# Order of high and low products within a quarter of a column tile, in a decoder layer on one Trainium2 core

## The chip, the cores and the metric

One core of a Trainium2 chip runs the whole kernel. TensorE multiplies, ScalarE (ACT) and VectorE (DVE) work element by element, GpSimd (POOL) takes a few element-wise steps and some DMAs, and SyncE (SP) issues most DMAs. The metric is the device time of one execution in microseconds (us); smaller is better.

## The reference, cut to what matters

One decoder layer on 256 tokens of 2048 numbers. A combined input projection gives latent queries, a shared key/value latent, gates, indexer queries and keys and the input of a recurrence; branch A is sparse attention with 16 heads, branch B a gated linear recurrence; both are projected, gated, added, projected once more, added to the input and normalised.

```python
proj = jnp.einsum('btd,dc->btc', x, w_in[l])
(q_lat, c_kv, attn_gate, q_idx, k_idx, w_idx,
 x_rnn, rnn_gate, g_a, g_b) = jnp.split(proj, SPLIT_POINTS, axis=-1)
...
attn = _sparse_attention(q_lat, c_kv, q_idx, k_idx, w_idx, rel_bias, w_uv[l])
branch_a = jnp.einsum('btc,cd->btd', attn * jax.nn.silu(attn_gate), w_branch_a[l])
h = _rglru(x_rnn, conv_w[l], conv_b[l], w_gate_a[l], b_gate_a[l], w_gate_x[l], b_gate_x[l], lru_lambda[l])
branch_b = jnp.einsum('btc,cd->btd', h * jax.nn.silu(rnn_gate), w_branch_b[l])
merged = jax.nn.sigmoid(g_a) * branch_a + jax.nn.sigmoid(g_b) * branch_b
sub = jnp.einsum('btd,de->bte', merged, w_out[l])
x = _layernorm(ALPHA * x + sub, ln_g[l], ln_b[l])
```

## The kernel before, in words

All numbers are float32. For the products each operand is written as a sum of a high and a low part of 12 significant bits each (`hi_of`, line 84, on ScalarE; `lo_of`, line 87, on VectorE). A product then is high x high + high x low + low x high. The activations of all 256 tokens stand as [high 256 | low 256], 512 columns, for each of the 16 slices k of the 2048 inputs: `xs[:, k, :]`, or `us[k]` for the two branch projections.

The large weights come as *column tiles*: 2048 rows (16 slices k of 128) by 128 columns. There are 148 of them, in the order of `col_jobs` (line 51): 4 of indexer queries (qi), 16 attention gates (ag), 32 queries (q), 16 + 16 of gate and projection of branch A (ga, ba), 16 recurrence inputs (xr), gates and recurrence gates (gb, rg), 16 of the projection of branch B (bb). A column tile arrives in two halves of 8 slices (`load_to`, line 148, DMAs of 512 KB on SP's queue); each half is split into hi and lo (`split_to`, line 161), with five buffers for each part.

The loop over column tiles (line 720) goes through four *quarters* of four slices each. For a slice, `mm3` (line 183) issues two products into one accumulator of 512 columns (`ps_...`, one of four banks): the weights' high part (stationary) times all 512 columns, and the weights' low part times the left 256 columns only. So the right half collects high x low, the left half high x high + low x high.

```python
        if last:
            nc.tensor.matmul(ps[:, :T], lo, rhs[:, :T], start=first, stop=False)
            nc.tensor.matmul(ps, hi, rhs, start=False, stop=True)
        else:
            nc.tensor.matmul(ps, hi, rhs, start=first, stop=False)
            nc.tensor.matmul(ps[:, :T], lo, rhs[:, :T], start=False, stop=False)
```

Behind each quarter stands `tick(t)` (line 112): it emits one more step of whatever other work is due, an agenda written by hand: the evacuation of finished tiles (`evac`, line 261: ScalarE copies the right half, VectorE adds the left), the indexer (products pss), attention heads (products psl, transposes pspT, products pspv), the heads' values (psv), the recurrence's gates (psg). Their TensorE products come between two quarters. Behind a first or third quarter the next half is split and a further half is loaded. The order on each engine is the order in which the program issues.

Ahead of the column tiles stands phase A (keys, latent, first indexer queries), which also uses `mm3` (line 257). Behind them stands the output projection (`products`, line 771): into pso and the first psz it issues 512-column products only, into the last psz 256-column ones only. Then come residual and norm.

Of the kernel before, what the change touches and what calls it, by code (L numbers as in the profile page):

```python
# [16 lines left out]
DRAM = bass.MemoryType.DRAM  # L17

P = 128
T = 256  # L20
DM = 2048
KT = DM // P
# [6 lines left out]
EPS = 1e-5  # L29
# [19 lines left out]


def col_jobs():
    """The column tiles in the order in which the tensor engine takes them."""
    jobs = [("qi", i) for i in range(4, 8)]
    jobs += [("ag", i) for i in range(16)]
    jobs += [("q", i) for i in range(2 * NH)]
    jobs += [("ga", i) for i in range(16)] + [("ba", i) for i in range(16)]
    jobs += [("xr", i) for i in range(16)]
    jobs += [("gb", i) for i in range(14)] + [("rg", i) for i in range(16)] + [("gb", 14), ("gb", 15)]
    jobs += [("bb", i) for i in range(16)]
    return jobs  # L60
# [3 lines left out]
def layer(ctx, tc, ar, out):  # L64
# [20 lines left out]
        nc.scalar.activation(hi, src, AF.Copy)  # L85

    def lo_of(lo, src, hi):
        """src = hi + lo exactly, each of 12 significant bits."""
        nc.vector.tensor_sub(lo, src, f(hi))  # L89

    def acc_tile(name):
# [11 lines left out]
    def gate_tile(name):  # L103
        return gt.tile([P, T], F32, name=name, tag="gate", bufs=32)

# [1 line left out]
    agenda = {}  # L107

    def spawn(t, gen):
# [7 lines left out]
                continue  # L117
            spawn(t + (wait or 1), gen)

# [1 line left out]
    zero = const.tile([P, P], mybir.dt.bfloat16, name="zero")  # L121
    nc.vector.memset(zero, 0.0)
    one = const.tile([P, 1], F32, name="one")
# [14 lines left out]
    dv = dram.tile([NH, VL], F32, name="dv")  # L138
    dz = dram.tile([P, NH, VL], F32, name="dz")

# [1 line left out]
    halves = [("t", j, s) for j in range(NJ) for s in range(2)]  # L142
    halves += [("o", ec, pc) for ec in range(4) for pc in range(8)]
    NO = 2 * NJ
# [36 lines left out]
            st["split"] += 1  # L181

    def mm3(ps, hi, lo, rhs, first, last):
        """hi x [hi | lo] into all columns of ps, lo x hi into the left ones."""
        if last:
            nc.tensor.matmul(ps[:, :T], lo, rhs[:, :T], start=first, stop=False)
            nc.tensor.matmul(ps, hi, rhs, start=False, stop=True)
        else:
            nc.tensor.matmul(ps, hi, rhs, start=first, stop=False)  # L189
            nc.tensor.matmul(ps[:, :T], lo, rhs[:, :T], start=False, stop=False)  # L190

    def mm6(o, pairs):
        """o (256 columns) = the sum over pairs of (hi, lo) stationary x (hi, lo) moving."""
        n = len(pairs)
        for i, ((sh, sl), (mh, ml)) in enumerate(pairs):
            nc.tensor.matmul(o, sh, mh, start=i == 0, stop=False)
            nc.tensor.matmul(o, sh, ml, start=False, stop=False)
            nc.tensor.matmul(o, sl, mh, start=False, stop=i == n - 1)

# [1 line left out]
    warm = aux_tile("warm")  # L201
    for i in range(32):
        nc.tensor.matmul(warm[:, :P], zero, zero, start=True, stop=True)
# [55 lines left out]
                split_to(k - 11)  # L259

    def evac(ps, name, dst=None):
        """Both halves of a product's accumulator, added."""
        r = tmp_tile(f"r_{name}", "r")
        nc.scalar.activation(r, ps[:, T:], AF.Copy)
        yield
        if dst is None:
            dst = tmp_tile(f"s_{name}", "s")
        nc.vector.tensor_add(dst, ps[:, :T], r)
        return dst

    def rsqrt(ssq, tmp, scale):
        """-2 / sqrt(ssq * scale + EPS): the table's root and a Newton step."""
        v, y, z = tmp
        nc.scalar.activation(z, ssq, AF.Sqrt, scale=scale, bias=eps)
        nc.vector.tensor_scalar(v, ssq, scale, EPS, op0=OP.mult, op1=OP.add)
        yield
        nc.vector.reciprocal(y, z)
        yield
        nc.vector.tensor_mul(z, y, y)
        nc.vector.tensor_mul(z, z, v)  # L280
        nc.vector.scalar_tensor_tensor(v, z, -3.0, y, op0=OP.add, op1=OP.mult)
        return v

    gt = ctx.enter_context(pool("gt"))

    # the keys that the tokens of tile 1 - r can see
    W = (T, P)

# [1 line left out]
    idx_stack = ExitStack()  # L290
    idx = idx_stack.enter_context(pool("idx", side="right"))
    ks = {}
# [48 lines left out]
            lo_of(cT[d][:, T:], ps[:, d, :], cT[d][:, :T])  # L341

    def post_qi(i, ps):
        """Two heads' queries: each has its high part on one half of the partitions and its low
        part on the other, for keys that stand on both."""
        s = yield from evac(ps, f"qi{i}")
        yield
        q = qis[i] = slot(f"qis{i}")
        heads = [(slice(0, DI), slice(DI, P), slice(0, T)), (slice(DI, P), slice(0, DI), slice(T, 2 * T))]
        for own, other, c in heads:  # L350
            hi_of(q[own, c], s[own, :])
        yield
        for own, other, c in heads:
            lo_of(q[other, c], s[own, :], q[own, c])

    def scores(i):
        """Of the first token tile only the first half of the keys is causal: the first two
        quarters of pss hold q x hi and q x lo of those keys."""
        q, k = qis[i], ks[0].rearrange("p (a s) -> p a s", a=2)
        pss = [aux_tile(f"pss{i}_{g}") for g in range(2)]  # L360
        for g in range(2):
            nc.tensor.matmul(pss[g][:, :T], q[:, g * T:g * T + P], k[:, :, :P], start=True, stop=True)
            for e in range(2):
                nc.tensor.matmul(pss[g][:, T:], q[:, g * T + P:(g + 1) * T], k[:, e, :], start=e == 0, stop=e == 1)
        yield
        rl = []
        for g in range(2):
            rl.append(idx.tile([P, 2 * T], F32, name=f"rl{i}_{g}", tag="rl", bufs=4))
            nc.scalar.activation(rl[g][:, P:T], pss[g][:, P:T], AF.Copy)
            nc.scalar.activation(rl[g][:, T:], pss[g][:, T:], AF.Relu)  # L370
        yield
        for g in range(2):
            nc.vector.tensor_add(rl[g][:, :P], pss[g][:, :P], rl[g][:, P:T])
        yield
        for g in range(2):
            nc.gpsimd.tensor_scalar(rl[g][:, :P], rl[g][:, :P], 0.0, None, op0=OP.max)
        for g in range(2):
            yield
            for t in range(2):
                h = 2 * i + g  # L380
                c = slice(0, W[1 - t])
                prev = causal[:, t, c] if h == 0 else score[t][:, c]
                nc.vector.scalar_tensor_tensor(score[t][:, c], rl[g][:, t * T:t * T + W[1 - t]], wi[:, t, h:h + 1],
                                               prev, op0=OP.mult, op1=OP.add)
# [18 lines left out]
            c = slice(0, wide[t])  # L403
            nc.vector.tensor_add(mask[:, 1 - t, c], score2[t][:, c], causal[:, t, c])

# [1 line left out]
    def rel():  # L407
        oh = idx.tile([32, VL], F32, name="oh")
        nc.sync.dma_start(oh, ar["onehot"])
# [19 lines left out]
            nc.gpsimd.tensor_add(b[:, r, :W[r]], b[:, r, :W[r]], mask[:, r, :W[r]])  # L429
        bias[h] = b  # L430

# [1 line left out]
    vs = {}  # L433

    def values(g):
# [18 lines left out]
        lo_of(lo, ps, hi)  # L454
        vs[g] = (hi, lo)

# [1 line left out]
    qs = {}  # L458

    def post_q(i, ps):  # L460
# [72 lines left out]
        yield  # L533
        lo_of(us[h][:, T:], u, us[h][:, :T])

# [1 line left out]
    gates = {}  # L537

    def post_ag(i, ps):
# [34 lines left out]
        yield  # L574
        lo_of(xs[:, d, T:], g, xs[:, d, :T])

# [1 line left out]
    def lru_consts():  # L578
        """c8 = 8 softplus(-lambda), nc8 = -c8; log1p by the series of artanh."""
        lam = params[:, 7, :]  # L580
        t = const.tile([P, 4, 16], F32, name="lru")
        m, e, z, q = (t[:, i, :] for i in range(4))
# [70 lines left out]
        nc.vector.tensor_mul(t[:, T:], t[:, T:], xc)  # L653

    def decay(n):
        """a = exp(-x) in place of r, 1 - a^2 = tanh(x) (1 + a^2), x = 8 r softplus(-lambda)."""
        r, w = ri[n][:, :T], v[:, n, :]
        nc.scalar.activation(w, r, AF.Tanh, scale=c8[:, n:n + 1])
        nc.scalar.activation(r, r, AF.Exp, scale=nc8[:, n:n + 1])
        yield  # L660
        a2 = tmp_tile(f"a2{n}", "u", 2)
        nc.scalar.activation(a2, r, AF.Square)
        yield
        nc.vector.scalar_tensor_tensor(w, a2, 1.0, w, op0=OP.add, op1=OP.mult)
# [28 lines left out]
    posts = {"qi": post_qi, "ag": post_ag, "q": post_q, "ga": post_ga, "ba": post_ba, "xr": post_xr,  # L693
             "rg": post_rg, "gb": post_gb, "bb": post_bb}

# [1 line left out]
    E0, D0, A0, C0, G0 = (4 * at[k, 0] for k in ("ag", "q", "ga", "xr", "gb"))  # L697
    spawn(0, post_a())
    for i in range(4):
# [16 lines left out]
        spawn(G0 + 50 + q, roots(q))  # L716
    FIN = 4 * at["bb", 4]

# [1 line left out]
    for j, (kind, i) in enumerate(jobs):  # L720
        rhs = us if kind in ("ba", "bb") else {k: xs[:, k, :] for k in range(KT)}
        ps = acc_tile(f"ps_{kind}{i}")
        for qt in range(4):
# [20 lines left out]
                for e in range(2):  # L744
                    nc.gpsimd.dma_start(y[e], ar["xres"][e * P:(e + 1) * P, :])
            hi, lo = parts[t // 2]
            for kk in range(4):
                k = qt * 4 + kk
                c = slice((k % 8) * P, (k % 8 + 1) * P)
                mm3(ps, hi[:, c], lo[:, c], rhs[k], k == 0, k == KT - 1)  # L750
            if qt % 2:
                parts.pop(t // 2)
            tick(t)
# [2 lines left out]
                load_to(t // 2 + 9)  # L756
        spawn(4 * j + 4, posts[kind](i, ps))

# [1 line left out]
    st6 = [fin.tile([P, 5, 6], F32, name=f"st{t}") for t in range(2)]  # L760
    mv = [fin.tile([P, 2], F32, name=f"mv{t}") for t in range(2)]
    tmp = [fin.tile([P, 4], F32, name=f"lt{t}") for t in range(2)]

    def piece(n):
        """The rows 2 d and 2 d + 1 (of 128) of w_out's column chunk, as (hi, lo) each."""
        p = parts[n]
        if isinstance(p, list):
            return p
        return [tuple(w[:, i * 512:(i + 1) * 512] for w in p) for i in range(2)]
# [18 lines left out]
            yield  # L788

    def normalise(t, ne):  # L790
        """(y - mean) g' (-2 / std) + b, with g' = -g / 2: most columns on the vector engine,
        the rest between the scalar and the Pool engine."""
        mean = mv[t][:, 0:1]
        nc.vector.bn_aggr(mv[t], st6[t][:, :ne, :])
        cuts = [slice(0, 384), slice(384, 896), slice(896, 1280), slice(1280, 1536)]
# [114 lines left out]
```

## Time and profile before

| | |
|---|---|
| median of 3 runs | 1050.54 us (1047.70 to 1051.33) |
| span of the profiled execution | 1046.6 us |
| its own time | not listed apart from the three runs, which lie 1.1 to 4.7 us above its span |
| TensorE busy | 1029.8 us, 98% of the span, 5944 products |
| TensorE weight loads (PEld) | 901.2 us, beside the products |
| VectorE busy | 709.3 us, 68% |
| ScalarE busy | 571.6 us, 55% |
| GpSimd busy | 87.4 us, 8% |
| DMA | 201.49 MB, mean 193 GB/s |

The span runs from the first instruction to the last. A product's time in the timeline is modelled from its start and overlaps the next product's; the distance from one start to the next is what it occupies TensorE for, and is called its *slot* below. A weight load (LDWEIGHTS, engine PEld) goes beside the product ahead. A row of the summary by stretches gives, for each engine, busy us and in brackets the number of instructions that begin in the stretch.

### The profile page before, as it was taken

To read this page: it belongs to the slowest core of one execution; us is meant where nothing else is said; L and a number is where in the kernel's file an instruction comes from. 1 tells how busy PE (TensorE), PEld (TensorE's weight loads), DVE (VectorE), ACT (ScalarE), POOL (GpSimd) and SP (SyncE) were. 2 spreads that over 40 slices of the span, in tenths; PEclk is the share of its full clock that TensorE was granted. 3 is DMA by queue.
4 is the path that set the end of the run, shared out by engine and by line. 5 is a ranking of instruction groups with operands and counts; after the bars stand their busy time and mean duration, and the time that the engine had idled before them with its cause. 6 is when DMAs were issued, how large, how long until landed. Compare 5 with 4: busy or idle time off the path is not lost.

```text
span 1046.6 us, 16107 instructions
## 1 busy us (share of the span) xinstructions
PE 1029.8 (98%) x5944; PEld 901.2 (86%) x5944; DVE 709.3 (68%) x1246; ACT 571.6 (55%) x989; POOL 87.4 (8%) x121
## 2 busy tenths in 40 slices
PE   8999999999999999999999999999999999999995
PEld 7988888888888888888888888888888888888885
DVE  4667586677677676545555788856577777675666
ACT  5666355555655657544444555578755545554341
POOL 1003211111111100000000000000230020000002
PEclk9999999999999999999999999999999999999998
DMA  8745856755656654656566766555656677656652
GB/s 275 262 145 178 288 180 218 235 174 177 191 170 183 191 163 145 196 182 194 185 184 186 218 188 191 163 174 187 180 186 191 188 266 261 195 186 186 197 162 81
DMA packets 60575, 201.49 MB, mean 193 GB/s; under 512 B 6577, under 2 KB 13617, under 8 KB 59857
## 3 DMA queue, kind: packets, MB, share of 16 engines
q1 hardware_dynamic: 59120, 190.89, 59.2%
q0 software_dynamic: 944, 8.88, 2.3%
q8 instruction: 47, 0.77, 0.3%
q10 hardware_dynamic: 432, 0.70, 0.2%
q14 instruction: 32, 0.25, 0.1%
HBM read 198.31 MB, written 6.32 MB: 196 GB/s over the span
## 4 chain that ended last, share of the span: by engine, by line
PE 92%; DVE 2%; DMA 2%; ACT 2%; issue 1%; POOL 0%; SPq 0%; DVEq 0%; ACTq 0%; POOLq 0%
PE ps_q L189 11%; PE ps_q L190 5%; PE ps_rg L189 5%; PE ps_ba L189 5%; PE ps_bb L189 5%; PE ps_gb L189 5%; PE ps_xr L189 5%; PE ps_ga L189 5%; PE ps_xr L190 3%; PE ps_gb L190 3%; PE ps_bb L190 3%; PE ps_ba L190 3%; PE ps_ga L190 3%; PE ps_rg L190 3%; PE pso L776 2%; PE pso L777 2%
## 5 line engine op out<-in xcount | busy, mean ns | idle before, releaser
L89 DVE TENSOR_TENSOR lo<-raw,hi 128x1024 fp32r<-128x1024 f32 x324 | 401.2, 1239 | 296.7 <-ACT hi L85 296.3
L85 ACT ACTIVATE hi<-raw 128x1024 fp32r<-128x1024 f32 x324 | 340.8, 1053 | 98.1 <-PE pso L778 29.7
L189 PE MATMUL ps_q<-xs,hi 128*128 128x512 f32 x480 | 172.0, 396 | 0.0
L190 PE MATMUL ps_q<-xs,lo 128*128 128x256 f32 x480 | 134.5, 280 | 0.0
L189 PEld LDWEIGHTS ps_q<-xs,hi 128*128 128x128 f32 x480 | 90.1, 188 | 18.0
L190 PEld LDWEIGHTS ps_q<-xs,lo 128*128 128x128 f32 x480 | 90.6, 189 | 1.5
L189 PE MATMUL ps_xr<-xs,hi 128*128 128x512 f32 x240 | 86.0, 398 | 0.0
L189 PE MATMUL ps_ga<-xs,hi 128*128 128x512 f32 x240 | 85.7, 398 | 0.0
L189 PE MATMUL ps_ag<-xs,hi 128*128 128x512 f32 x240 | 85.6, 397 | 0.0
L189 PE MATMUL ps_gb<-xs,hi 128*128 128x512 f32 x240 | 85.6, 398 | 0.0
L189 PE MATMUL ps_ba<-ua,hi 128*128 128x512 f32 x240 | 85.4, 399 | 0.0
L189 PE MATMUL ps_rg<-xs,hi 128*128 128x512 f32 x240 | 85.4, 399 | 0.0
L189 PE MATMUL ps_bb<-ub,hi 128*128 128x512 f32 x240 | 85.4, 399 | 0.0
L190 PE MATMUL ps_ag<-xs,lo 128*128 128x256 f32 x240 | 67.6, 282 | 0.7 <-DVE lo L89 0.6
L190 PE MATMUL ps_xr<-xs,lo 128*128 128x256 f32 x240 | 67.4, 281 | 0.0
L190 PE MATMUL ps_gb<-xs,lo 128*128 128x256 f32 x240 | 67.4, 281 | 0.0
L190 PE MATMUL ps_ba<-ua,lo 128*128 128x256 f32 x240 | 67.4, 281 | 0.0
L190 PE MATMUL ps_rg<-xs,lo 128*128 128x256 f32 x240 | 67.4, 281 | 0.0
L190 PE MATMUL ps_bb<-ub,lo 128*128 128x256 f32 x240 | 67.4, 281 | 0.0
L190 PE MATMUL ps_ga<-xs,lo 128*128 128x256 f32 x240 | 67.3, 281 | 0.0
L189 PEld LDWEIGHTS ps_rg<-xs,hi 128*128 128x128 f32 x240 | 45.1, 188 | 10.4
L189 PEld LDWEIGHTS ps_ba<-ua,hi 128*128 128x128 f32 x240 | 45.1, 188 | 10.4
(306 smaller groups left out, 2091.3 us busy)
## 6 DMA issues: line engine op xcount, KB each, us to landing
raw<-in_wt SPq DMA_DIRECT2D x296, 512.0 KB, 4.1
raw<-in_wo SPq DMA_DIRECT2D x32, 512.0 KB, 4.3
wr<-in_wA SPq DMA_DIRECT2D x15, 424.0 KB, 4.9
dz<-dv POOLq DMA_DIRECT2D x1, 4096.0 KB, 18.8
bias<-dz SPq DMA_DIRECT2D x16, 256.0 KB, 4.4
xr<-in_xT SPq DMA_DIRECT2D x16, 128.0 KB, 4.7
uvr<-in_wuv SPq DMA_DIRECT2D x8, 256.0 KB, 4.1
wgr<-in_wg SPq DMA_DIRECT2D x4, 512.0 KB, 4.8
```

Source lines behind the costliest of these rows:

```text
L85: nc.scalar.activation(hi, src, AF.Copy)
L89: nc.vector.tensor_sub(lo, src, f(hi))
L189: nc.tensor.matmul(ps, hi, rhs, start=first, stop=False)
L190: nc.tensor.matmul(ps[:, :T], lo, rhs[:, :T], start=False, stop=False)
L776: nc.tensor.matmul(o, mh, hi, start=d == 0, stop=False)
L777: nc.tensor.matmul(o, mh, lo, start=False, stop=False)
```

## The change

In the loop over column tiles a new function `mm12` takes the place of the four calls of `mm3`. It issues the same eight products of a quarter, grouped by part: in the first and third quarter of a tile the four high products, then the four low ones; in the second and fourth the four low ones, then the four high ones. The accumulator is opened by the high product of slice 0 and closed by the high product of slice 15, as before. Phase A keeps `mm3`. Besides that only comments and docstrings are gone, so line numbers move by 13 or less.

```diff
+    def mm12(ps, hi, lo, rhs, qt):
+
+
+        def some(w, cols):
+            for k in range(4 * qt, 4 * qt + 4):
+                c = slice((k % 8) * P, (k % 8 + 1) * P)
+                nc.tensor.matmul(ps[:, :cols], w[:, c], rhs[k][:, :cols], start=k == 0 and w is hi,
+                                 stop=k == KT - 1 and w is hi)
+
+        order = [(hi, 2 * T), (lo, T)]
+        for w, cols in order if qt % 2 == 0 else order[::-1]:
+            some(w, cols)
+
...
             hi, lo = parts[t // 2]
-            for kk in range(4):
-                k = qt * 4 + kk
-                c = slice((k % 8) * P, (k % 8 + 1) * P)
-                mm3(ps, hi[:, c], lo[:, c], rhs[k], k == 0, k == KT - 1)
+            mm12(ps, hi, lo, rhs, qt)
             if qt % 2:
                 parts.pop(t // 2)
             tick(t)
```

On TensorE, the first quarter of the first tile of branch A's projection (ba0; ua0 to ua3 are the activations of slices 0 to 3, hi136 and lo136 the two parts of the weight half), in the program before:

```order
L189 MATMUL ps_ba0_5417<-ua0_2518,hi136_5327 128x512
L190 MATMUL ps_ba0_5417<-ua0_2518,lo136_5328 128x256
L189 MATMUL ps_ba0_5417<-ua1_2686,hi136_5327 128x512
L190 MATMUL ps_ba0_5417<-ua1_2686,lo136_5328 128x256
L189 MATMUL ps_ba0_5417<-ua2_2866,hi136_5327 128x512
L190 MATMUL ps_ba0_5417<-ua2_2866,lo136_5328 128x256
L189 MATMUL ps_ba0_5417<-ua3_3026,hi136_5327 128x512
L190 MATMUL ps_ba0_5417<-ua3_3026,lo136_5328 128x256
```

and now:

```order
L198 MATMUL ps_ba0_5417<-ua0_2518,hi136_5327 128x512
L198 MATMUL ps_ba0_5417<-ua1_2686,hi136_5327 128x512
L198 MATMUL ps_ba0_5417<-ua2_2866,hi136_5327 128x512
L198 MATMUL ps_ba0_5417<-ua3_3026,hi136_5327 128x512
L198 MATMUL ps_ba0_5417<-ua0_2518,lo136_5328 128x256
L198 MATMUL ps_ba0_5417<-ua1_2686,lo136_5328 128x256
L198 MATMUL ps_ba0_5417<-ua2_2866,lo136_5328 128x256
L198 MATMUL ps_ba0_5417<-ua3_3026,lo136_5328 128x256
```

The eight products are the same; the low ones have moved behind the four high ones.

The end of that tile and the start of the next (ba1), before:

```order
L189 MATMUL ps_ba0_5417<-ua13_4673,hi137_5352 128x512
L190 MATMUL ps_ba0_5417<-ua13_4673,lo137_5353 128x256
L189 MATMUL ps_ba0_5417<-ua14_4808,hi137_5352 128x512
L190 MATMUL ps_ba0_5417<-ua14_4808,lo137_5353 128x256
L186 MATMUL ps_ba0_5417<-ua15_4930,lo137_5353 128x256
L187 MATMUL ps_ba0_5417<-ua15_4930,hi137_5352 128x512
L189 MATMUL ps_ba1_5468<-ua0_2518,hi138_5378 128x512
L190 MATMUL ps_ba1_5468<-ua0_2518,lo138_5379 128x256
L189 MATMUL ps_ba1_5468<-ua1_2686,hi138_5378 128x512
L190 MATMUL ps_ba1_5468<-ua1_2686,lo138_5379 128x256
```

and now:

```order
L198 MATMUL ps_ba0_5417<-ua12_4519,lo137_5353 128x256
L198 MATMUL ps_ba0_5417<-ua13_4673,lo137_5353 128x256
L198 MATMUL ps_ba0_5417<-ua14_4808,lo137_5353 128x256
L198 MATMUL ps_ba0_5417<-ua15_4930,lo137_5353 128x256
L198 MATMUL ps_ba0_5417<-ua12_4519,hi137_5352 128x512
L198 MATMUL ps_ba0_5417<-ua13_4673,hi137_5352 128x512
L198 MATMUL ps_ba0_5417<-ua14_4808,hi137_5352 128x512
L198 MATMUL ps_ba0_5417<-ua15_4930,hi137_5352 128x512
L198 MATMUL ps_ba1_5468<-ua0_2518,hi138_5378 128x512
L198 MATMUL ps_ba1_5468<-ua1_2686,hi138_5378 128x512
L198 MATMUL ps_ba1_5468<-ua2_2866,hi138_5378 128x512
L198 MATMUL ps_ba1_5468<-ua3_3026,hi138_5378 128x512
```

Before, two products of one size stand together only here; now four low and then eight high ones do.

A whole tile of the recurrence inputs now (equal rows are counted together; xs are the activations of all slices):

```order
L198 MATMUL ps_xr_6327<-xs,hi_6235 128x512 x4
L198 MATMUL ps_xr_6327<-xs,lo_6236 128x256 x8
L198 MATMUL ps_xr_6327<-xs,hi_6235 128x512 x4
L198 MATMUL ps_xr_6327<-xs,hi_6260 128x512 x4
L198 MATMUL ps_xr_6327<-xs,lo_6261 128x256 x8
L198 MATMUL ps_xr_6327<-xs,hi_6260 128x512 x4
```

Before, such a tile was 15 times a high and a low product in turn, and a low and a high one at its end. Products of other work that `tick` emits between the first and second or the third and fourth quarter now stand between two groups of four low products, those between the second and third, or behind the fourth, between two groups of four high ones.

## Rows read from the trace of the kernel before

**Rows 1.** The page: busy time of the engines (part 1), chain by engine (part 4).
```profile
PE 1029.8 (98%) x5944; PEld 901.2 (86%) x5944; DVE 709.3 (68%) x1246; ACT 571.6 (55%) x989; POOL 87.4 (8%) x121
...
PE 92%; DVE 2%; DMA 2%; ACT 2%; issue 1%; POOL 0%; SPq 0%; DVEq 0%; ACTq 0%; POOLq 0%
```

**Rows 2.** Summary by stretches, 427 to 947 us: all instructions, then those of psg alone.
```profile
core 0: us, PE busy (x) PEld busy (x) DVE busy (x) ACT busy (x) POOL busy (x), PEclk, DMA share, GB/s
427.00:947.00 520.00, 520.00 (x2976) 452.52 (x2975) 353.80 (x519) 287.31 (x452) 25.65 (x35) 1.00 0.63 194
...
427.00:947.00 520.00, 14.12 (x96) 12.55 (x96) 13.33 (x32) 1.00 0.63 194
```

**Rows 3.** Timeline (start us, us, engine, line) at a tile's end, TensorE.
```profile
500.26 0.28 PE L186 MATMUL ps_ba<-ua,lo 128*128 128x256 f32 x1
...
500.38 0.40 PE L187 MATMUL ps_ba<-ua,hi 128*128 128x512 f32 x1
...
500.61 0.40 PE L189 MATMUL ps_ba<-ua,hi 128*128 128x512 f32 x1
...
500.85 0.28 PE L190 MATMUL ps_ba<-ua,lo 128*128 128x256 f32 x1
500.85 0.19 PEld L189 LDWEIGHTS ps_ba<-ua,hi 128*128 128x128 f32 x1
500.96 0.40 PE L189 MATMUL ps_ba<-ua,hi 128*128 128x512 f32 x1
...
501.67 0.40 PE L189 MATMUL ps_ba<-ua,hi 128*128 128x512 f32 x1
```

**Rows 4.** Timeline, TensorE, one column tile and the next one's first product.
```profile
140.19 0.40 PE L189 MATMUL ps_ag<-xs,hi 128*128 128x512 f32 x1
...
140.90 0.39 PE L189 MATMUL ps_ag<-xs,hi 128*128 128x512 f32 x1
...
145.06 0.39 PE L189 MATMUL ps_ag<-xs,hi 128*128 128x512 f32 x1
...
145.75 0.39 PE L189 MATMUL ps_ag<-xs,hi 128*128 128x512 f32 x1
```

**Rows 5.** By tile pso (ns min/median/max, first and last start); timeline of psz.
```profile
L776 PE MATMUL pso<-hi,xs x96: 389/389/396, 947.4 to 1012.0; 128*128 128x512 f32 x96
...
1028.16 0.28 PE L778 MATMUL psz<-hi,xs 128*128 128x256 f32 x1
...
1029.36 0.28 PE L776 MATMUL psz<-wh,xs 128*128 128x256 f32 x1
```

**Rows 6.** Summary 169.1:387.0 (same columns): all, ps_q, psl, psv, pspv, pspT.
```profile
169.10:387.00 217.90, 217.90 (x1341) 194.51 (x1340) 154.12 (x361) 128.15 (x271) 29.07 (x35) 1.00 0.62 189
...
169.10:387.00 217.90, 186.72 (x1024) 156.45 (x1023) 12.81 (x31) 11.37 (x31) 1.00 0.62 189
...
169.10:387.00 217.90, 18.88 (x140) 17.53 (x140) 8.73 (x28) 3.90 (x14) 1.00 0.62 189
...
169.10:387.00 217.90, 11.50 (x84) 10.33 (x84) 4.77 (x7) 4.19 (x7) 1.00 0.62 189
...
169.10:387.00 217.90, 9.80 (x52) 7.96 (x52) 5.02 (x12) 4.76 (x13) 1.00 0.62 189
...
169.10:387.00 217.90, 6.38 (x39) 4.81 (x39) 7.99 (x26) 7.19 (x26) 1.00 0.62 189
```

**Rows 7.** Timeline, TensorE: first transpose of a head, second product behind them.
```profile
209.60 0.27 PE L504 MATMUL pspT<-ident,lg 128*128 128x128 f32 x1
...
210.16 0.28 PE L190 MATMUL ps_q<-xs,lo 128*128 128x256 f32 x1
```

**Rows 8.** Timeline at 131 us: VectorE's low part, TensorE around it.
```profile
130.58 1.23 DVE L89 TENSOR_TENSOR lo<-raw,hi 128x1024 fp32r<-128x1024 f32 x1 [0.84 <-ACT hi L85]
...
130.84 0.40 PE L189 MATMUL ps_ag<-xs,hi 128*128 128x512 f32 x1
...
131.86 0.39 PE L190 MATMUL ps_ag<-xs,lo 128*128 128x256 f32 x1 [0.63 <-DVE lo L89]
```

## The prediction

> **What bounds the kernel now.** I read the page first, then stretches of it, then single products. The page shows TensorE busy for 98% of the span, and PE as 92% of the chain that ended last; VectorE and ScalarE are busy for 68% and 55% [rows 1]. So the end moves with TensorE's pace. The summary by stretches says how fast that is: from 427 to 947 us TensorE starts 2976 products in 520.00 us without a gap, at clock 1.00, the 2.4 GHz level [rows 2]. 96 of them are the gate products psg, the other 2880 are 1440 pairs of one 512-column product (high part) and one 256-column product (low part).
>
> The timeline then gives the slot of one product, from its start to the next one's start (the 0.40 us in a row is a modelled duration and overlaps the next). In that long stretch three pairs take 501.67 - 500.61 = 1.06 us, 353.3 ns a pair [rows 3]. But the same pairs, earlier in the program, also run at another pace: from 140.90 to 145.06 twelve pairs take 4.16 us, 346.7 ns a pair, at the same clock and with the same instructions [rows 4]. And where products of one size follow each other, the slots are the short ones: the output projection's 512-column products take (1012.0 - 947.4) us over 95 rounds of three, 226.7 ns each, its 256-column products 1.20 us for ten, 120.0 ns each [rows 5]; together 346.7 ns, the fast pace. So some 6.7 ns a pair are lost in the alternating stream, most of the time but not always. VectorE works 353.80 of the 520 us and ScalarE 287.31 [rows 2], so the supply of split weights doesn't explain it.
>
> **The change, part by part.** No product, weight load, DMA or split is added or removed; inside a quarter (four pairs) the four high products come first and the four low ones after, in the next quarter low first. No queue but TensorE's is reordered. Neighbours of equal size become the rule: per column tile the stream goes from 512 to 256 columns and back twice in place of 15 times.
>
> *Late stretch, 427 to 947 us.* The gate products take 96 x 0.120 = 11.5 us, which leaves 508.5 us for 1440 pairs, 353.1 ns each [rows 2]. At 346.7 ns they take 499.2 us: 9.3 us can go. This is the main term.
>
> *Stretch of the queries, 169.1 to 387.0 us.* There are 512 pairs (ps_q, 1024 products), 140 + 84 products of 256 columns (psl, psv), 13 groups pspv of one 512 and three 256, and 39 transposes pspT [rows 6]. At the short slots that is 177.5 + 26.9 + 13 x 0.587 = 7.6, in all 212.0 us. Three transposes and the high product after them take 210.16 - 209.60 = 0.56 us [rows 7], so without that product 0.33, for 13 groups 4.3. Of the 217.9 us 1.6 are left: this stretch already runs mostly at the fast pace. I take 1.0 of it, between 0 and 1.6.
>
> *Stretch before it (gates ag).* Here TensorE waits for others now and then. One such wait: the product of the high part starts at 130.84, the next, with the low part, only at 131.86, since VectorE made that low part from 130.58 to 131.81 [rows 8]. In place of a slot of 0.23 this cost 1.02, so 0.79 us. With the change three more high products stand before the first low one: the low part is needed 3 x 0.227 = 0.68 us later and most of this wait goes. I take 1.3 us for the stretch, 0.6 for the wait and 0.7 for pace; between 0 (VectorE, busy with the indexer, just makes TensorE wait elsewhere) and 3.
>
> *What is kept.* Two round trips between sizes remain in each of 148 tiles; if each still costs the 6.7 ns of a pair, 2.0 us. A tile at the fast pace takes 145.75 - 140.19 = 5.56 us against 16 x 0.3467 = 5.547 [rows 4], so its ends cost some 13 ns that the slow tiles' even 353.3 ns hide: 1.2 us over the 90 tiles of the late stretch. Together 3.2; the bounds are 0 and 3.2.
>
> *Costed at nothing.* Weight loads: each begins with the product before it (the load for the high part at 500.85, together with the low product) [rows 3]. In a run of low products each load has only a 120 ns slot to hide under; the projection's run of 256-column products does the same at 120.0 ns [rows 5], so the cover is there. Accumulating several times in a row into the same bank is what that projection does too. The high parts' buffers are read until the end of their half, 0.12 us later than before, the low parts' are free about 0.9 us sooner; five buffers of each make that nothing. If a half came late after all, the DMA would be late next: it is at 63% of its engines [rows 2]. The last products of a tile are high ones before and after, so what follows a tile starts the same.
>
> Sum: -9.3 - 1.0 - 1.3 + 3.2 = -8.4 us on the span of 1046.6 us. The page doesn't give the profiled execution's own time; the three runs lie 1.1 to 4.7 us above the span, their median 3.9. On that median: 1050.5 - 8.4 = **1042.1 us**, 0.8% less. Bounds of the terms: gains of 9.3 + 1.6 + 3 with nothing kept give 1036.6.
>
> **The rivals.** *The order makes no difference.* The pace would belong to the stretch, not to the order: two equal neighbours would then inherit the slow slots. For it: at a tile's end two high products already stand together, and their slots are 500.61 - 500.38 = 0.23 and 0.24, not 0.227, although the two low ones before them take 0.12 [rows 3]; and the slow tile is an even 16 x 353.3 ns with no discount for that spot. Against it: the fast pace occurs in the very same tiles, so 226.7 + 120.0 is open to them, and every long run of one size in the trace has it [rows 4, 5]. Time 1050.5, give or take 1.5. The Trainium skill ("TensorE: Matmul & The Clock Gate", section "Back-to-back issue gap") has a rule on this side: a slot follows from the product's own columns, N/2.4 + 2.5 ns. By that rule the sum would be zero; the trace disagrees with it as far as one and the same pair is seen at 346.7 and at 353.3 ns.
>
> *Slower: the longer slots take over everywhere.* The extra inserted products of the query stretch seem to throw the stream back into the fast pace. If runs of four keep the slow slot for high products (0.2355, the mean of the two at the tile's end) and pay 0.120 for each low one, a pair costs 355.5 ns: 1440 x 2.4 ns = 3.5 us more in the late stretch, and the 512 pairs of the queries, now near 346.7, lose up to 8.8 ns each, 4.5 us. That gives 1054 (late stretch alone) to 1058.5. It decides from a mean pair of 354.6 ns on (353.3 and 3.2 us over the 2368 pairs of the 148 tiles). Against it stands that this price rests on single slots beside a change of tile.
>
> *The gain starves.* Pairs get shorter, but the early stretches or a late DMA turn that into waits; a gain of 3.5 to 5 us, 1046. VectorE's free third in the late stretch speaks against more than that.
>
> **How the numbers follow.** Forecast 0.62 (gain 5 to 13 us); starved 0.10; no difference 0.15; slower 0.13. The runs of before spread over 3.6 us, so a change under about 0.3% (3.2 us) can't be told from none. Faster 0.72, same 0.15, slower 0.13. The range goes from the bounds of the terms to just past no difference: 1036.5 to 1051.5; it leaves out the slower case and little else.
>
> **What would show it.** Right: in the ba to bb tiles high slots of 227 ns and low ones of 120 within the runs, a column tile of 5.56 to 5.58 us in place of 5.65, the 427 to 947 stretch some 8 us shorter, TensorE's busy time about 8 us lower with the share unchanged, and the lo wait in the ag tiles gone. Wrong: high slots of 233 or more inside a run (no difference, or slower with low slots of 120), new waits of TensorE on hi or lo (starved), or the query stretch longer than 218 us (longer slots everywhere).

## The result and the profile after

The changed kernel takes 1039.89 us (median of 4 runs, 1039.49 to 1041.05) against 1050.10 us (4 runs, 1047.70 to 1051.33): ratio 0.9912, 95% interval 0.9897 to 0.9927. It is faster by 0.9%, inside the forecast range and 2.2 us below the forecast 1042.1. The profiled execution took 1039.67 us, 1.9 us more than its span of 1037.8 us.

The page, parts 1 and 4, answers to [rows 1]:

```profile
PE 1021.8 (98%) x5944; PEld 901.4 (87%) x5944; DVE 709.8 (68%) x1246; ACT 571.1 (55%) x989; POOL 86.3 (8%) x121
...
PE 92%; DMA 3%; DVE 2%; ACT 1%; issue 1%; POOL 0%; SPq 0%; DVEq 0%; ACTq 0%; POOLq 0%
```

The same 5944 products, the same 98% of the span, 8.0 us less of it: TensorE still sets the end and goes quicker. Where, is read from the first starts of four tiles (engine, duration ns min/median/max, first and last start us), by tile, of the kernel before:

```profile
L189 PE MATMUL ps_qi<-xs,hi x60: 387/395/476, 47.1 to 69.8; 128*128 128x512 f32 x60
...
L189 PE MATMUL ps_q<-xs,hi x480: 387/395/475, 169.1 to 386.3; 128*128 128x512 f32 x160
...
L189 PE MATMUL ps_ga<-xs,hi x240: 387/398/481, 387.0 to 482.9; 128*128 128x512 f32 x120
```

and of the changed one (for pso before see [rows 5]):

```profile
L198 PE MATMUL ps_qi<-xs,hi x64: 389/393/477, 46.6 to 69.6; 128*128 128x512 f32 x64
...
L198 PE MATMUL ps_q<-xs,hi x512: 389/393/478, 167.6 to 384.5; 128*128 128x512 f32 x171
...
L198 PE MATMUL ps_ga<-xs,hi x256: 389/393/478, 384.7 to 480.4; 128*128 128x512 f32 x128
...
L786 PE MATMUL pso<-hi,xs x96: 389/389/393, 938.6 to 1003.2; 128*128 128x512 f32 x96
```

| from the first product of ... to that of ... | before | after | gain |
|---|---|---|---|
| qi to q (gates ag among them) | 122.0 us | 121.0 us | 1.0 |
| q to ga | 217.9 | 217.1 | 0.8 |
| ga to the output projection | 560.4 | 553.9 | 6.5 |
| all column tiles | 900.3 | 892.0 | 8.3 |

The projection itself, 64.6 us from first to last row of pso, is as before. What the span lost beyond 8.3 lies ahead of the column tiles, where the start of the first one moves from profile to profile (47.1, 46.6, and 45.3 to 50.3 in the profiles below); so single spans and times differ by some us, and I read the experiments by their column tiles.

In the summary by stretches, late stretch (columns as in [rows 2], then psg alone), 96 x 0.120 us for psg leave 501.5 us for 1438 pairs, 348.7 ns each, against 353.1:

```profile
424.00:937.00 513.00, 513.00 (x2972) 452.91 (x2971) 353.43 (x517) 286.20 (x450) 25.79 (x35) 1.00 0.63 197
...
424.00:937.00 513.00, 14.02 (x96) 12.55 (x96) 13.32 (x32) 1.00 0.63 197
```

The timeline of TensorE in a tile of ba answers to [rows 3] (runs of equal products stand in one row, with the first start):

```profile
492.74 1.12 PE L198 MATMUL ps_ba<-ua,lo 128*128 128x256 f32 x8
493.69 2.00 PE L198 MATMUL ps_ba<-ua,hi 128*128 128x512 f32 x8
495.53 1.12 PE L198 MATMUL ps_ba<-ua,lo 128*128 128x256 f32 x8
496.48 1.32 PE L198 MATMUL ps_ba<-ua,hi 128*128 128x512 f32 x5
```

Eight low products take 0.95 us, 119 ns each; eight high ones 1.84 us, 230 ns each, not 227. From start to start the eight high slots are 233, 236, 228, 233, 231, 227, 226 and 227 ns, and the first low one behind them 113: 20 ns over the floor in each round trip, 40 in a tile of 5587 ns.

### The profile page after: what moved, and what is told of

The parts are those of the page before. It is cut to its first block, busy times and chain, and to the rows that moved or that the text cites. A ratio compares the mean times of both kernels' runs of the same rounds, so it can differ in the third digit from the quotient of the medians.

```text
span 1037.8 us, 16087 instructions
## 1 busy us (share of the span) xinstructions
PE 1021.8 (98%) x5944; PEld 901.4 (87%) x5944; DVE 709.8 (68%) x1246; ACT 571.1 (55%) x989; POOL 86.3 (8%) x121
## 4 chain that ended last, share of the span: by engine, by line
PE 92%; DMA 3%; DVE 2%; ACT 1%; issue 1%; POOL 0%; SPq 0%; DVEq 0%; ACTq 0%; POOLq 0%
PE ps_q L198 17%; PE ps_ga L198 9%; PE ps_bb L198 9%; PE ps_rg L198 9%; PE ps_ba L198 9%; PE ps_gb L198 9%; PE ps_xr L198 9%; PE ps_ag L198 4%; DMA raw<-in_wt 3%; PE ps_qi L198 2%; PE pso L788 2%; PE pso L787 2%; PE pso L786 2%; ACT hi L85 1%; PE psq L189 1%
## 5 line engine op out<-in xcount | busy, mean ns | idle before, releaser
L198 PE MATMUL ps_q<-xs,hi 128*128 128x512 f32 x512 | 133.6, 394 | 0.0
L198 PE MATMUL ps_q<-xs,lo 128*128 128x256 f32 x512 | 73.5, 282 | 0.0
L198 PE MATMUL ps_xr<-xs,hi 128*128 128x512 f32 x256 | 64.0, 391 | 0.0
L198 PEld LDWEIGHTS ps_bb<-ub,hi 128*128 128x128 f32 x256 | 46.0, 189 | 8.2
L198 PEld LDWEIGHTS ps_gb<-xs,hi 128*128 128x128 f32 x256 | 46.0, 189 | 8.2
L198 PEld LDWEIGHTS ps_xr<-xs,hi 128*128 128x128 f32 x256 | 46.0, 188 | 8.0
L198 PEld LDWEIGHTS ps_ag<-xs,hi 128*128 128x128 f32 x256 | 45.3, 189 | 8.5 <-issue 0.9
L198 PEld LDWEIGHTS ps_ga<-xs,hi 128*128 128x128 f32 x256 | 45.6, 189 | 7.7
L442 POOL TENSOR_TENSOR bias<-bias,mask 128x256 f32<-128x256 f32 (+1 forms) x32 | 25.9, 830 | 174.8 <-DMA bias<-dz 136.2
L198 PEld LDWEIGHTS ps_xr<-xs,lo 128*128 128x128 f32 x256 | 35.8, 190 | 2.5
```

The lines of the kernel that those rows point to most:

```text
L198: nc.tensor.matmul(ps[:, :cols], w[:, c], rhs[k][:, :cols], start=k == 0 and w is hi, stop=k == KT - 1 and w is hi)
```

## The experiments

Tile lengths below are of tiles with no other products inside (plain tiles), in the late stretch; they and single slots in ns are start-to-start distances in the trace, which the views round to 10 ns. They can be read from two rows by tile, the first starts of ba and xr, 16 tiles apart; for the changed kernel (570.0 - 480.7) / 16 = 5.58 us. The floor is 16 x (226.7 + 120.0) = 5547 ns. Ratios are to the kernel before, run beside the experiment on the same chip.

**Runs of another length.** First order: two high, two low, two high, two low in a quarter.

```diff
+        for k0 in (4 * qt, 4 * qt + 2):
+            for w, cols in ((hi, 2 * T), (lo, T)):
+                for k in (k0, k0 + 1):
```

> Order in a quarter: two high, two low, two high, two low (8 round trips between sizes per column tile). Theory S (each of the first three high products behind a low one carries 6.7 ns over 226.7 ns, low ones take 120): all 16 high products carry it, a plain tile of the late stretch stays at 5653 ns, the time at 1048 to 1051 us. Rival C (every round trip between sizes costs the 20 ns seen in the changed kernel): 8 x 20 ns, tile 5707 ns, about 1057 us. Rival D (every round trip costs the 6.7 ns of the alternating stream): 8 x 6.7 ns, tile 5600 ns, about 1042 us.

Second, the changed kernel without the turn:

```diff
-        for w, cols in order if qt % 2 == 0 else order[::-1]:
+        for w, cols in order:
```

> The changed kernel without the turn: every quarter has four high, then four low products (4 round trips per tile, the low part needed as late as in the changed kernel). S: 12 of 16 high products carry 6.7 ns, tile 5627 ns, about 1046 us. C: 4 x 20 ns, the same 5627 ns. D: 4 x 6.7 ns, tile 5573 ns, about 1038 us. Rival W (the gain comes from the low part being needed later): as the changed kernel, about 1040 us.

Third, eight high, sixteen low and eight high in a tile:

```diff
+        w, cols = (hi, 2 * T) if qt in (0, 3) else (lo, T)
+        for k in range(8 * (qt // 2), 8 * (qt // 2) + 8):
```

> Per tile eight high, sixteen low, eight high products, so one round trip and runs of sixteen. S and C: 20 ns over the floor of 5547, tile 5567 ns, 3 us less than the changed kernel, about 1037 us. D: tile 5553 ns, 5 us less than the changed kernel, about 1035 us. If the cost grows with the length of the runs: tile 5587 ns, no gain over the changed kernel, 1040 us.

And the changed kernel again:

> The changed kernel once more beside the others, for the comparison on one chip: every theory expects a plain tile of 5587 ns and 1038 to 1042 us.

| order | ratio (interval) | column tiles, us | late tile, ns | over the floor | round trips |
|---|---|---|---|---|---|
| before | 1 | 900.3 | 5653 | 107 | 15 |
| runs of two | 0.9912 (0.9892 to 0.9933) | 892.2 | 5573 | 27 | 8 |
| runs of four | 0.9962 (0.9947 to 0.9976) | 894.8 | 5613 | 67 | 4 |
| changed, again | 0.9929 (0.9908 to 0.9950) | 892.9 | 5587 | 40 | 2 |
| eight and sixteen | 0.9902 (0.9884 to 0.9919) | 890.6 | 5567 | 20 | 1 |

By tile, first ba then xr, runs of two:

```profile
L197 PE MATMUL ps_ba<-ua,hi x256: 393/396/398, 480.6 to 569.3; 128*128 128x512 f32 x128
...
L197 PE MATMUL ps_xr<-xs,hi x256: 393/396/398, 569.8 to 667.8; 128*128 128x512 f32 x128
```

and runs of eight and sixteen:

```profile
L196 PE MATMUL ps_ba<-ua,hi x256: 389/389/398, 479.1 to 568.0; 128*128 128x512 f32 x128
...
L196 PE MATMUL ps_xr<-xs,hi x256: 389/389/398, 568.2 to 666.3; 128*128 128x512 f32 x128
```

From runs of four on a round trip costs 17 to 20 ns, near the 20 that S and C both expected there. Runs of two refute S (5653), C (5707) and D (5600) alike: their high slots stay at 231 to 236 ns, but their low ones fall to 112 to 119, so a round trip costs 3.3 ns. With 15 of them in a tile it costs 7 ns, with 8 of them 3, with 4 of them 17, with 2 or 1 of them 20: my picture of a fixed loss at each change of size was wrong. W as the whole cause is refuted by runs of four: the low part is needed as late as in the changed kernel, and from ga to the output projection the gain is 3.7 us, not 6.5.

The changed kernel again has the tile of 5587 ns and the queries' 217.1 us, but from qi to q it takes 122.0 us, as long as before. That stretch's gain of 1.0 us is not shown to belong to the change.

**One part alone.** The tiles are split at the seventh ga tile.

```diff
-            mm12(ps, hi, lo, rhs, qt)
+            if t >= A0 + 24:
+                mm12(ps, hi, lo, rhs, qt)
+            else:
...
+                    mm3(ps, hi[:, c], lo[:, c], rhs[k], k == 0, k == KT - 1)
```

This is the late part alone; the early part alone has `t < A0 + 24` in its place.

> Groups as in the changed kernel from the seventh ga tile to the end of bb, alternation as before in all tiles ahead of it. Theory S2 (the gain is the slot pace of the alternating products, wherever they run at 353.3 ns a pair): 90 of 148 tiles carry it, 90 x (5653 - 5587) ns = 6.0 us of the 8.3 that the column tiles gained, about 1044 us; the tiles ahead as before. Rival W (the gain comes from low parts being needed later, in the tiles where TensorE waited): nothing here, 1050 us.

> The complement: groups in the tiles qi, ag, q and the first six ga, alternation in the 90 tiles behind. S2: 1.8 to 2.4 us less than before, 1047 to 1048 us, with the late stretch of plain tiles at 5653 ns. W: the whole gain, 1040 to 1042 us.

Measured: late only 1042.81 us, ratio 0.9924 (0.9909 to 0.9940), column tiles 894.2 us; early only 1048.19 us, ratio 0.9976 (0.9967 to 0.9986), column tiles 899.3. Of the 8.3 us, 6.1 came with the late tiles, as S2 had it, and 1.0 with the early ones, 0.8 us short of S2's lower end; 1.2 us came with neither; from qi to q alone the two profiles of the changed kernel differ by 1.0. W, with the whole gain early, is refuted again.

**Sizes or parts.** The low part's products are taken over all 512 columns, so a part of the sum is computed that the kernel before leaves out. This also takes the turned last pair away, and the closing product of a tile is a low one.

```diff
-                mm3(ps, hi[:, c], lo[:, c], rhs[k], k == 0, k == KT - 1)
+                nc.tensor.matmul(ps, hi[:, c], rhs[k], start=k == 0, stop=False)
+                nc.tensor.matmul(ps, lo[:, c], rhs[k], start=False, stop=k == KT - 1)
```

> The kernel before with the low part's products taken over all 512 columns too (this adds low x low, which the reference's sum contains and the kernel before leaves out, to the right half): the parts still alternate, the sizes don't. If the change of size costs the time: all slots 226.7 ns, a plain tile 32 x 226.7 = 7253 ns, in all 1.6 us a tile more than the floor, about 1278 us. If the change from part to part costs it (6.7 ns a pair): 7360 ns, 1294 us. If a high product of this stream simply takes 233.3 ns: 7467 ns, 1310 us.

Measured: one run of 1289.66 us, plain tiles of 7253 ns, as the first case had it. (The 1278 us beside it was mis-added: 1.6 us is the excess over the tile of before, not over the floor, and 1050.5 + 148 x 1.6 = 1287.) Going from part to part costs nothing where sizes are equal. The timeline of that kernel, at 227 ns a slot:

```profile
599.89 0.39 PE L750 MATMUL ps_ba<-ua,hi 128*128 128x512 f32 x1
600.11 0.39 PE L751 MATMUL ps_ba<-ua,lo 128*128 128x512 f32 x1
600.34 0.39 PE L750 MATMUL ps_ba<-ua,hi 128*128 128x512 f32 x1
600.57 0.39 PE L751 MATMUL ps_ba<-ua,lo 128*128 128x512 f32 x1
```

**The turned last pair.** This is the experiment that decided. The kernel before issues the last slice of a tile as low, then high, so that two low and then two high products stand together once per tile. Here that is undone, so a low product closes the accumulator, and nothing else changed: sizes alternate through all tile ends.

```diff
-                mm3(ps, hi[:, c], lo[:, c], rhs[k], k == 0, k == KT - 1)
+                nc.tensor.matmul(ps, hi[:, c], rhs[k], start=k == 0, stop=False)
+                nc.tensor.matmul(ps[:, :T], lo[:, c], rhs[k][:, :T], start=False, stop=k == KT - 1)
```

> The kernel before without the turned last pair: high and low alternate through tile ends too, so no two equal neighbours stand in the stream of column tiles. Theory S2 (alternating sizes lose 6.7 ns a pair by themselves): plain tiles stay at 5653 ns, about 1050 us. Rival H (the pair of equal neighbours at a tile's end throws the stream into the long slots, and it would stay at 346.7 ns a pair without it): plain tiles of 5547 to 5560 ns wherever no other products come between, 1036 to 1040 us.

> The same kernel as pure_alternation once more, in other executions. If the products of the last attention heads always put the stream into the short pattern: plain late tiles of 5547 ns again, 10 to 13 us less than before. If the pattern of an execution is chance: late tiles of 5653 ns in this profile, or single times near 1045 us and above.

Measured: 1038.13 us, ratio 0.9878 (0.9862 to 0.9894), and again 1040.35 us, ratio 0.9910 (0.9887 to 0.9932); column tiles 890.5 and 890.1 us; all plain late tiles 5547 ns in both profiles, the floor, with sixteen round trips each. S2 falls, H holds: alternation of sizes costs nothing by itself. The timeline shows four pairs in 488.07 - 486.69 = 1.38 us, 345 ns each (346.7 over a tile); a high slot is 230 ns here and a low one 117, not the 227 and 120 of runs of one size:

```profile
486.69 0.39 PE L750 MATMUL ps_ba<-ua,hi 128*128 128x512 f32 x1
486.92 0.28 PE L751 MATMUL ps_ba<-ua,lo 128*128 128x256 f32 x1
...
488.07 0.39 PE L750 MATMUL ps_ba<-ua,hi 128*128 128x512 f32 x1
```

Its plain ag tiles, though, and the first queries stay at 5649 to 5661 ns; behind the first products of an attention head the next plain tile takes 5547 ns, in both profiles. So both patterns occur without a turned pair. What makes them last was tried with a single turned pair, at the end of the first ba tile:

```diff
+                both = [(hi, 2 * T), (lo, T)]
+                if k == KT - 1 and j == 68:
+                    both = both[::-1]
```

> Pure alternation with a single turned last pair (low, then high), at the end of the first tile of ba. Theory T (in an alternating stream either pattern of slots, 346.7 or 353.3 ns a pair, goes on until something disturbs it; the turned pair of the kernel before puts it into the longer one): plain tiles of 5547 ns ahead of that spot and of 5653 ns behind it, 80 tiles x 0.107 = up to 8.5 us more than pure alternation, about 1045 us. Rival L (a turn costs only at its own place, and the stream recovers): 5547 ns again within a tile, 1038 us.

Measured: 1040.59 us, ratio 0.9920 (0.9899 to 0.9942). The timeline around the turned pair (486.78 and 487.02 are the rows of two):

```profile
484.82 0.39 PE L754 MATMUL ps_ba<-ua,hi 128*128 128x512 f32 x1
...
486.55 0.39 PE L754 MATMUL ps_ba<-ua,hi 128*128 128x512 f32 x1
486.78 0.40 PE L754 MATMUL ps_ba<-ua,lo 128*128 128x256 f32 x2
487.02 0.62 PE L754 MATMUL ps_ba<-ua,hi 128*128 128x512 f32 x2
487.48 0.28 PE L754 MATMUL ps_ba<-ua,lo 128*128 128x256 f32 x1
487.60 0.40 PE L754 MATMUL ps_ba<-ua,hi 128*128 128x512 f32 x1
...
489.37 0.40 PE L754 MATMUL ps_ba<-ua,hi 128*128 128x512 f32 x1
```

Five pairs ahead of it take 1.73 us (346 ns each), five behind it, from 487.60 to 489.37, 1.77 us (354 ns). All eleven plain tiles ahead, from the seventh ga to the first ba, are 5546 to 5550 ns long, and the 18 tiles behind 5645 to 5661; then the first gate products psg come, and two tiles later the stream is at 346.7 ns again and stays there to the end. So T's mechanism is shown, that either pattern goes on by itself, and its size was off: the longer pattern lasted for 18 tiles, not 80. The length of the ba stretch says the same: (572.0 - 481.7) / 16 = 5.64 us here, against (574.4 - 485.6) / 16 = 5.55 us without the pair (first two rows pure_alternation, then one_turned_pair):

```profile
L750 PE MATMUL ps_ba<-ua,hi x256: 391/391/391, 485.6 to 574.0; 128*128 128x512 f32 x128
...
L750 PE MATMUL ps_xr<-xs,hi x256: 390/391/391, 574.4 to 672.1; 128*128 128x512 f32 x128
...
L754 PE MATMUL ps_ba<-ua,hi x256: 391/398/403, 481.7 to 571.7; 128*128 128x512 f32 x128
...
L754 PE MATMUL ps_xr<-xs,hi x256: 390/391/403, 572.0 to 670.2; 128*128 128x512 f32 x128
```

The longer pattern is not an even 353.3 ns. It is a cycle of three pairs, of 236 + 113, 232 + 118 and 241 + 120 ns (some by 1 ns less or more), 1060 ns in all. In the kernel before, behind the 501.67 of [rows 3], the pairs so take 0.35, 0.35 and 0.36 us:

```profile
502.02 0.40 PE L189 MATMUL ps_ba<-ua,hi 128*128 128x512 f32 x1
...
502.37 0.40 PE L189 MATMUL ps_ba<-ua,hi 128*128 128x512 f32 x1
...
502.73 0.40 PE L189 MATMUL ps_ba<-ua,hi 128*128 128x512 f32 x1
```

What followed a turned pair went by its place in this cycle. The 15 pairs ahead of it in a tile of the kernel before are five cycles, so from 427 us on all 89 turned pairs between two tiles come behind a third pair, and the longer pattern goes on each time. Earlier, seven came behind a second pair, and the shorter pattern followed; the tile of [rows 4] begins behind one of these. Of the turned pairs that met the even slots of the shorter pattern, 12 led to the longer one and one, at 145.4 us, did not.

Is it the tile's end or the order of four neighbours? The pair was turned at slice 7 instead (`if k == 7`):

> Alternation with the turned pair (low, then high) at the eighth slice of every tile, not at the last. T with the order of four neighbours (low, low, high, high) as the cause: plain late tiles of 5653 ns, about 1049 us. If it needs the change of accumulator or the closing product at the tile's end: 5547 to 5560 ns, about 1038 us.

Measured: 1047.27 us, ratio 0.9982 (0.9968 to 0.9997), plain late tiles of 5653 ns. The order low, low, high, high does it, without any change of accumulator or closing product. The 16 tiles with gate products take 6280 ns here, 6373 before: behind the gate products, which come behind a first pair of the cycle, the stream goes on in the shorter pattern, three pairs in 599.50 - 598.46 = 1.04 us:

```profile
597.39 0.40 PE L754 MATMUL ps_xr<-xs,hi 128*128 128x512 f32 x1
...
597.75 0.28 PE L196 MATMUL psg<-xcs,wgh 128*128 128x256 f32 x1
...
598.46 0.39 PE L754 MATMUL ps_xr<-xs,hi 128*128 128x512 f32 x1
...
599.50 0.39 PE L754 MATMUL ps_xr<-xs,hi 128*128 128x512 f32 x1
```

In the kernel before they come behind 12 pairs, four cycles, and in all 16 tiles the longer pattern goes on behind them. So it does behind the first ones of one_turned_pair, which come behind a third pair (three pairs in 595.03 - 593.97 = 1.06 us); the next ones there come behind a first pair, and the shorter pattern follows:

```profile
592.88 0.40 PE L754 MATMUL ps_xr<-xs,hi 128*128 128x512 f32 x1
...
593.25 0.28 PE L196 MATMUL psg<-xcs,wgh 128*128 128x256 f32 x1
...
593.97 0.39 PE L754 MATMUL ps_xr<-xs,hi 128*128 128x512 f32 x1
...
595.03 0.40 PE L754 MATMUL ps_xr<-xs,hi 128*128 128x512 f32 x1
```

Last, runs of eight and sixteen ahead of the seventh ga tile and alternation without turned pairs behind it, by the same test on t as above:

> Runs of eight and sixteen up to the sixth ga tile, pure alternation behind. T: the late tiles have whichever pattern the stream enters with: 5547 ns (then about 1036 us, 1 to 2 us less than pure alternation and the runs of eight and sixteen) or 5653 ns (then about 1046 us), but not a mixture in plain tiles. Rival A (alternation after grouped tiles is always short): 1036 us.

Measured: 1039.17 us, ratio 0.9906 (0.9889 to 0.9924), column tiles 891.8 us. The alternating part enters with the longer pattern, keeps it through 29 tiles of 5640 to 5661 ns, and goes over to 5547 at the first gate products, which come behind a second pair. Rival A is refuted. T's forecast, one pattern and no mixture, fails; its mechanism holds, as each pattern goes on until other products come.

## Why the prediction was right, and where it was not

*What bounds, and where it shows.* Right: TensorE's slots set the end, 98% busy before and after, and no other engine took over; VectorE's share is 68% in both.

*The main term.* Forecast 9.3 us in the late stretch, 6.9 net of what is kept in its 90 tiles; measured 6.5 from ga to the projection, with 40 of the 107 ns a tile left. Right in place and sign.

*What is kept.* This term was too small: 2 x 6.7 ns and 13 ns for a tile's ends make 27 ns, measured 40. The price of a round trip was taken from the alternating stream; in runs of eight it is 20 ns, spread over the first five high products, and a tile's ends cost nothing beyond it. So of the signs one meant as wrong, high slots of 233 or more inside a run, did show, on three of each eight high products; and the tile of 5587 ns lies just past the 5.56 to 5.58 us named as right.

*Queries and ag.* For the queries 1.0 was forecast, 0.6 net of what is kept in 32 tiles, and 0.8 measured (twice). For the stretch before them it was 1.3, net 1.0, and 1.0 was measured and, in the second profile, 0.0. Of the waits of the kernel before

```profile
PE ps_ag L190 <- DVE lo L89: 0.6, 1, 0.6
PE pss L362 <- DVE rl L373: 0.6, 1, 0.6
```

the one on the low part did leave TensorE's list, which now holds no row of ps_ag:

```profile
PE psc L266 <- DVE alo L89: 1.7, 2, 1.0
PE psc L265 <- ACT ahi L85: 1.1, 1, 1.1
PE warm L216 <- DVE eps L127: 1.0, 1, 1.0
PE pss L375 <- DVE rl L386: 0.8, 1, 0.8
```

but the one on the indexer's rl grew to 0.8 us, and in the second profile a wait on a high part stands beside it:

```profile
PE ps_ag L198 <- ACT hi L85: 0.3, 1, 0.3
```

The sum, 8.4 against a measured 8.3, agrees because small errors stood against each other, 0.4 us too much in the late stretch and 0.2 too little for the queries; the 7.4 of the second profile lack the gain ahead of the queries.

*The cause.* Here the prediction was wrong, in the step "Neighbours of equal size become the rule", which made the alternation of sizes the price. Alternation runs at 346.7 ns a pair through all plain late tiles of pure_alternation, 29 and 45 on end. The stream has two patterns of slots that go on by themselves, and in the late stretch the turned pairs held the kernel before in the longer one: each restarted its cycle, and so the gate products, too, came at a place where they do not end it. The change gained because it broke that alternation up and so left both patterns, not because size changes are dear. That the number came out is luck as far as this goes: the sum needed only the two measured paces, 353.1 ns before and 346.7 in runs of one size, and any reason for the difference that spares runs of one size would have given it. The row that told it stood in the first rival: the two high products at a tile's end with slots of 0.23 and 0.24 us, read there as a sign for no difference. That rival's own reading, that a pace belongs to its stretch, was nearer to the mechanism than mine; it failed only in carrying the pace over to runs of one size.

*The slower rival.* It carried the longer high slots of the tile's end into runs of four. In runs of four without the turn they do appear, 224 to 236 ns, and a tile there is 26 ns longer than in the changed kernel; but with low slots of 116 to 120 it is still 40 ns shorter than before.

*The starved rival.* The only new wait of TensorE on hi or lo in the lists above is the 0.3 us of the second profile; DMA stays at 63% of its engines.

*Products with slots of their own.* In one_turned_pair the same products in the same order take 346 ns a pair ahead of one turned pair and 354 behind it, so a slot isn't set by its product alone. The Trainium skill ("TensorE: Matmul & The Clock Gate", section "Back-to-back issue gap") gives N/2.4 + 2.5 ns, a figure of the product's own columns, as the gap of an isolated product. As a rule for every slot of this stream, as the prediction read it, it is contradicted by that.

## What to carry to other kernels

Where a stream of products of mixed sizes is the bound, read start-to-start distances over a whole tile, and compare stretches of one kernel with each other: the same instructions at two paces, as here, can mean that something upstream in the order sets the pace. Then undo the irregular spot first; here taking one turned pair per tile away gave as much as regrouping everything (1038.1 and 1040.4 us against 1039.9 and 1042.1, with column tiles 1.5 to 2.8 us shorter, which the intervals of the ratios don't separate safely). Runs of eight and sixteen give as much (890.6 us of column tiles), and their plain tiles take 5566 or 5567 ns early and late alike, where those of alternation take 5547 or 5649 to 5661 by what came before.

## What the runs showed of the hardware that was not expected

- An alternating stream of 512- and 256-column products, each with its own weight load, runs at 346.7 or 353.3 ns a pair at the granted clock 1.00, and kept either until other products came: 29 tiles (928 products, grouped_then_alternating) in the longer, 45 tiles to the end of the stream (pure_alternation) in the shorter. The longer one is a cycle of three pairs, 1060 ns.
- A turned pair (two low, two high neighbours) turned the shorter into the longer one in one_turned_pair, and in the late stretch of turned_pair_in_the_middle behind each group of gate products. In the longer one its effect went by its place in the cycle: behind a third pair the longer went on (98 of 98 in the kernel before), behind a second the shorter followed (7 of 7).
- Six gate products of 256 columns left the longer pattern as it was behind a third pair (16 of 16 in the kernel before) and led to the shorter behind a first or second one (16 of 16 in turned_pair_in_the_middle, once each in two other runs). The indexer's six products pss, also of 256 columns, differ: five times in pure_alternation they come behind a second pair, and each time the longer pattern is back by the next tile (behind the last of them two plain tiles of 5649 and 5650 ns).
- Behind a run of 256-column products five 512-column ones in a row have longer slots (233, 236, 228, 233, 231 ns) before they settle at 227.

Which unit of the chip holds these patterns no run here shows; weight loads begin with the product ahead in both of them. No run moved the gate products by themselves: that their place in the cycle decides is read from tiles of several kernels.
